# A threshold search on one NeuronCore: two bits a round on three engines, or one bit a round on ScalarE

## The chip, the cores and the metric

The kernel runs on one core of a Trainium2 chip. A core has TensorE (PE; its weight loads are listed as PEld), VectorE (DVE), ScalarE (ACT), GpSimd (POOL) and SyncE (SP), which issues most DMAs. Each engine takes its instructions in the order in which they were put at compile time, and waits at an instruction until what it needs is there. The metric is the device time of one execution in microseconds (us); the time before is the median of three.

## The reference, cut to what matters

One decoder layer for a prompt of 1024 tokens and 8 sample sequences of 4 new tokens. Each sample query picks 256 of its 8192 cached positions and 4 new ones by an indexer's score, and attends only to these:

```python
s = jnp.einsum('bqhd,bsd->bqhs', qi, ki) * (D_IDX ** -0.5)
score = jnp.einsum('bqh,bqhs->bqs', wi, jax.nn.relu(s))
score = jnp.where(valid, score, -jnp.inf)
top_val, top_idx = lax.top_k(score, topk)        # topk = 256
...
kg = flat_k[phys_row]; vg = flat_v[phys_row]     # gather the chosen keys and values
o = softmax(q @ kg + bias) @ vg
```

Beside this branch stand the prompt's own top-256 attention, a retention branch (eight heads, chunks of 128 tokens), the gates, the output projection, and a gated per-layer embedding. All of it is in fp32.

## The kernel before

The kernel is one stream of work in about five stages: norm and indexer projections; the remaining projections with the indexer scores of prompt and sample; the retention branch (a loop over four pairs of heads, `hp` 0 to 3, lines 1361 to 1418); the attention branch (a loop over eight query blocks `qb`, lines 1471 to 1531); and the output projections. The order on each engine is made at compile time: a scheduler goes through the program with estimated durations and gives an engine, when it comes free, the ready instruction of the highest priority. Work that is traced inside `tc.high_priority()` goes ahead of what is ready beside it. The order is fixed then; on the chip an engine waits if its next instruction is not ready.

The part that the change touches is `bisect_sample` (`bss`), which finds for each of the 32 sample queries the 256th largest score. The scores of a query lie on four partitions, 2080 columns each (tile `Xt`, `NX` = 2080). Their upper 16 bits are turned into unsigned keys (`su`, in the code `u16`), a first search finds the upper 16 bits of the threshold, the keys are then made from the lower 16 bits, and a second search finds these. A search of `before` goes through 8 rounds of two bits. In a round three thresholds are counted:

- two by ScalarE (`signs`, line 844): an ACTIVATE with `Sign` over all 2080 columns, its threshold as bias, and the sum of the signs into a column of `sgn`;
- the middle one by VectorE (line 883), in three pieces of 704, 688 and 688 columns, each followed by a small instruction (line 887) that carries the sum on;
- TensorE adds up the four partitions of a query with one small matmul of `groupr` and `sgn` (`totals`, line 849; the result is `stot`);
- ScalarE takes the signs of the three totals (line 893, with their sum in `up`) and makes the next two thresholds from `up` and two prepared values `pre` (line 865); GpSimd prepares those (line 870), and VectorE updates the middle one (line 894).

So a round is a chain ACT and DVE, PE, ACT, and the next round cannot start before it. Between the searches stands one more count with one pass (line 907). After the searches come two counts on VectorE (lines 836 and 928), each with a total on TensorE.

What follows on the threshold is `sample_select` (`ss`): it compares all scores with it, ranks them by scans, and in eleven steps of three queries (lines 1179 to 1199; tile `psl`) makes the row numbers `idx` of the chosen keys from step functions `oh`. The gathers (line 1086) fetch those rows, and `sample_attn` (`sa`) attends to them, interleaved with the prompt's attention by `more`, which sets its pace. All of `bss` and `ss` is traced with high priority, from `steps`, which stands after each projection block of the retention loop:

```python
with tc.high_priority():
    step(bss if hp == 0 else ss)
if hp == 0:
    step(bp, 2)
```

A generator's `yield` ends a step. `bss` yields after every round; what is left of it at `hp` 1 is traced at once. `bp` is the prompt's own threshold search, whose last part (scans and masks of the six query blocks, lines 698 to 712) runs on VectorE while the sample search starts. The small results `stot` share one PSUM bank that is kept over the retention and the attention stage (`kept`, tags `t` and `s`).

Of the kernel before, what the change touches and what calls it, by code (L numbers as in the profile page):

```python
# [10 lines left out]
F32 = mybir.dt.float32  # L11
F32R = mybir.dt.float32r
BF16 = mybir.dt.bfloat16
I32 = mybir.dt.int32
U16 = mybir.dt.uint16
AF = mybir.ActivationFunctionType
ALU = mybir.AluOpType
# [5 lines left out]
NS = 32  # L23
# [93 lines left out]
CW = _CW["onehot"][0]  # L117
# [3 lines left out]
def tile_step(ctx: ExitStack, tc: tile.TileContext, I, O):  # L121
    nc = tc.nc
# [21 lines left out]
    def bank(name, tag="b"):  # L144
        if tag in kept.get("tags", ()):
            return kept["pool"].tile([128, 512], F32, tag="s", bufs=1, name=name)
        return psum["pool"].tile([128, 512], F32, tag=tag, bufs=psum["bufs"][tag], name=name)
# [568 lines left out]
    def step(gen, n=1):  # L716
        for _ in range(n):
            next(gen, None)
# [49 lines left out]
    for b in range(8):  # L768
        rls = []
        for a in range(2):  # L770
# [4 lines left out]
            for up in range(2):  # L775
# [9 lines left out]
                for u2 in range(2):  # L785
                    nc.tensor.matmul(po[u2 * 64:u2 * 64 + 64, :], qbd[:, b, :], kT[:, u2 * 512:u2 * 512 + 512],  # L786
                                     start=True, stop=True)
# [16 lines left out]
    NX = 2048 + NS  # L804
    stk = ExitStack()

    def bisect_sample():


        V = nc.vector  # L810
        ss_ = stk.enter_context(pool("sst", side="right"))
        Xt = ss_.tile([128, NX], F32, name="Xt")
        u16 = ss_.tile([128, NX], U16, name="su16")
        jk = ss_.tile([128, NX], BF16, name="sjk")
# [5 lines left out]
        nc.gpsimd.memset(Xt[:, 2048:], LOW)  # L820
        V.tensor_copy(Xt[:NS, 2048:], newsc)
        bits = ss_.tile([128, 2], I32, name="sbits")
        nc.sync.dma_start(jk.bitcast(F32)[:, :128], I["const"][:, CW + 384:CW + 512])
        groupr = ss_.tile([128, 128], F32R, name="groupr")
        nc.gpsimd.tensor_copy(groupr, jk.bitcast(F32)[:, :128])
        group = groupr.bitcast(F32)
        cand, gb = (bits[:, i:i + 1] for i in range(2))
        sm = ss_.tile([128, 11], F32, name="ssm")
        cnt, sg, ng, c65, tu, v, need, te, k1, k2, bias = (sm[:, i:i + 1] for i in range(11))
        sgn = ss_.tile([128, 4], F32R, name="sgn")  # L830
        ct = cand.bitcast(F32)
        q1 = slice(0, NS)

        def count(thr, op):

            V.tensor_scalar(jk, Xt, thr, None, op0=op, op1=ALU.add, accum_out=cnt)
            t = bank("stot", "t")[:, 0:1]
            nc.tensor.matmul(t, group, cnt, start=True, stop=True)
            return t

        def signs(src, bias, j):

            with nc.allow_low_precision(reason="whole numbers up to NX"):
                nc.scalar.activation(jk, src, AF.Sign, bias=bias, accum_out=sgn[:, j:j + 1])  # L844

        def totals():

            t = bank("stot", "t")[:, 0:4]
            nc.tensor.matmul(t, groupr, sgn, start=True, stop=True)
            return t  # L850

        def search(src, k, mid):


            s = float(1 << 14)
            b = None
            V.memset(mid, 2 * s - 0.5)
            pre = ss_.tile([128, 4], F32, tag="pre", bufs=2, name="pre")
            for j in range(2):
                nc.gpsimd.memset(pre[:, j:j + 1], 0.5 - (3 - 2 * j) * s)  # L860
            for r in range(8):
                if r:
                    b = pre[:, 2:4]
                    for j in range(2):
                        nc.scalar.activation(b[:, j:j + 1], up, AF.Identity, bias=pre[:, j:j + 1], scale=-2.0 * s)
                        signs(src, b[:, j:j + 1], j)
                    if r < 7:
                        pre = ss_.tile([128, 4], F32, tag="pre", bufs=2, name="pre")
                        for j in range(2):
                            nc.gpsimd.tensor_scalar(pre[:, j:j + 1], b[:, j:j + 1], 0.75 * s * (1 - 2 * j), None,  # L870
                                                    op0=ALU.add)
                else:
                    for j in range(2):
                        signs(src, pre[:, j:j + 1], j)
                    p0, pre = pre, ss_.tile([128, 4], F32, tag="pre", bufs=2, name="pre")
                    for j in range(2):
                        nc.gpsimd.tensor_scalar(pre[:, j:j + 1], p0[:, j:j + 1], 0.75 * s * (1 - 2 * j), None,
                                                op0=ALU.add)
                c2 = ss_.tile([128, 5], F32, tag="c2", bufs=2, name="c2")
                part = -float(NX)  # L880
                for j, c, w in ((0, 0, 704), (1, 704, 688), (2, 1392, 688)):
                    jv = ss_.tile([128, 704], BF16, tag="jv", bufs=1, name="jv")
                    V.tensor_scalar(jv[:, :w], src[:, c:c + w], mid, None, op0=ALU.is_ge, op1=ALU.add,
                                    accum_out=c2[:, j:j + 1])
                    to = c2[:, 3 + j:4 + j] if j < 2 else sgn[:, 2:3]
                    with nc.allow_low_precision(reason="whole numbers up to NX"):
                        V.tensor_scalar(to, c2[:, j:j + 1], 2.0, part, op0=ALU.mult, op1=ALU.add)
                    part = to
                t = totals()

                st = ss_.tile([128, 4], F32, tag="st4", bufs=2, name="st4")
                up = st[:, 3:4]
                nc.scalar.activation(st[:, 0:3], t[:, 0:3], AF.Sign, bias=k, accum_out=up)
                V.scalar_tensor_tensor(mid, up, s / 2, mid, op0=ALU.mult, op1=ALU.add)
                s /= 4
                yield

        hi16 = Xt.bitcast(U16).rearrange("p (n two) -> p n two", two=2)
# [3 lines left out]
        V.tensor_scalar(lw, hi16[:, :, 1], float(1 << 15), float((1 << 15) - 1), op0=ALU.is_ge, op1=ALU.mult)  # L902
        V.scalar_tensor_tensor(u16, lw, 1 << 15, hi16[:, :, 1], op0=ALU.bitwise_xor, op1=ALU.bitwise_xor)  # L903
        yield
        yield from search(u16, k1, tu)
        V.tensor_scalar(bias, tu, -1.0, -0.5, op0=ALU.mult, op1=ALU.add)
        signs(u16, bias, 0)
        t = totals()[:, 0:1]
        V.tensor_scalar(k2, t, float(8 * NX - 2 * TOPK + 1), None, op0=ALU.add)
        V.tensor_scalar(ng, tu, float(1 << 15), None, op0=ALU.is_lt)  # L910
        V.tensor_scalar(c65, ng, 65535.0, None, op0=ALU.mult)
# [4 lines left out]
        V.tensor_scalar(ng, ng, 98303.0, -32768.0, op0=ALU.mult, op1=ALU.add)  # L916
        V.scalar_tensor_tensor(tu, tu, sg, ng, op0=ALU.mult, op1=ALU.add)
        yield
        yield from search(u16, k2, v)
        V.scalar_tensor_tensor(v, v, sg, c65, op0=ALU.mult, op1=ALU.add)  # L920
        V.tensor_copy(cand, tu)
        V.tensor_copy(gb, v)
# [2 lines left out]
        tot = count(ct, ALU.is_gt)  # L925
# [1 line left out]

        V.tensor_scalar(jk[:, :2048], Xt[:, :2048], ct, None, op0=ALU.is_equal, op1=ALU.add, accum_out=cnt)
        tot = bank("stot", "t")[:, 0:1]
        nc.tensor.matmul(tot, group, cnt, start=True, stop=True)  # L930
        V.tensor_copy(te, tot)
        tf = ct[q1]
        need, te = need[q1], te[q1]
        for src, dst in ((tf, tq), (need, nq)):
            t = bank("tbc", "t")
            nc.tensor.transpose(t[:, :NS], src.to_broadcast([NS, 128]), ident[:NS, :NS])
            V.tensor_copy(dst, t[:, :NS])
        xn = Xt[:NS, 2048:]
        sel, eq, rk = (jk.bitcast(F32)[:NS, i * NS:i * NS + NS] for i in range(3))
        V.tensor_scalar(sel, xn, tf, None, op0=ALU.is_gt)  # L940
        V.tensor_scalar(eq, xn, tf, None, op0=ALU.is_equal)
        V.tensor_tensor_scan(rk, eq, eq, te, op0=ALU.add, op1=ALU.bypass)
# [6 lines left out]
    bss = bisect_sample()  # L949
# [390 lines left out]
    ss = sample_select()  # L1340
# [13 lines left out]
    def steps(hp):  # L1354

        with tc.high_priority():
            step(bss if hp == 0 else ss)
        if hp == 0:
            step(bp, 2)

    for hp in range(4):
# [24 lines left out]
        for tb in range(8):  # L1386
# [3 lines left out]
            vv, sg = take_vg(pt, 128, tb, hp, f"{hp}_{tb}")  # L1390
            sgs.append(sg)
            qk = qks[tb]
            r, qkT, sm = chunk_mm(qk, vv, tb, 128, tri, hp)
# [77 lines left out]
    for qb in range(8):  # L1471
# [4 lines left out]
        w = min(n, 256)  # L1476
# [266 lines left out]
```

## Time and profile before

| | |
|---|---|
| time, median of 3 runs | 1080.19 us (1079.3 to 1080.88) |
| profiled execution, its own time | 1084.95 us |
| its span in the profile | 1083.1 us |
| TensorE busy, matmuls | 1005.3 us, 93% |
| VectorE, ScalarE, GpSimd busy | 765.1, 572.4, 292.4 us |
| mean granted TensorE clock | 0.964 of full speed |

All rows come from the one profiled execution; its time is 4.76 us above the median of the runs. An engine's busy share over the span is a mean over stages: the windows below show stretches of the span by themselves. Idle time matters where the engine that sets the end is the idle one.

### The profile page before, as it was taken

What the parts mean: (1) busy time and instruction counts of PE and PEld (TensorE: products, weight loads), DVE (VectorE), ACT (ScalarE), POOL (GpSimd) and SP (SyncE); (2) the same over time, 40 slices, a digit from 0 to 9 for tenths busy, and PEclk for the clock granted to TensorE, in tenths of its full rate; (3) what the DMA queues carried; (4) which work ended last, traced back from release to release, by engine and by line L of the source; (5) the groups of instructions that cost most, each with busy time, mean ns of one, the idle gap of its engine ahead of it and who ended that gap; (6) DMA issues with size and microseconds to landing.
All of it is one profiled execution on the core that took longest, in us unless ns stands there. A gap on an engine that the chain in (4) does not pass through costs nothing.

```text
span 1083.1 us, 20067 instructions
## 1 busy us (share of the span) xinstructions
PE 1005.3 (93%) x7377; PEld 845.4 (78%) x7377; DVE 765.1 (71%) x2262; ACT 572.4 (53%) x1216; POOL 292.4 (27%) x301
## 2 busy tenths in 40 slices
PE   3899997988998889999999986899999799999998
PEld 2899997766776788888888954566665799999998
DVE  6847778989889998968769879677663622683332
ACT  5545564976798356877832335555554432442210
POOL 3102223111201532424425215544331421122110
PEclk9999999989999999999999975899999899999999
DMA  8211235536343311300321544434211511332211
GB/s 285 65 59 50 78 107 176 180 116 203 125 161 103 74 40 40 80 18 26 79 81 25 141 119 110 133 87 115 58 50 61 144 60 40 115 125 81 84 41 41
DMA packets 98308, 102.24 MB, mean 94 GB/s; under 512 B 21346, under 2 KB 88386, under 8 KB 95906
## 3 DMA queue, kind: packets, MB, share of 16 engines
q1 hardware_dynamic: 92450, 74.74, 23.2%
q0 software_dynamic: 5760, 26.22, 7.8%
q8 instruction: 58, 0.95, 0.4%
q14 instruction: 40, 0.33, 0.1%
HBM read 79.25 MB, written 21.68 MB: 93 GB/s over the span
## 4 chain that ended last, share of the span: by engine, by line
PE 67%; DVE 14%; issue 6%; ACT 6%; DMA 4%; POOL 2%; SPq 0%; POOLq 0%; DVEq 0%; ACTq 0%
PE pb L252 4%; PE pb L253 4%; PE pb L254 4%; PE pg L262 3%; PE pg L264 3%; PE pg L263 3%; PE ob L1519 3%; PE ptp L1511 2%; PE pvg L262 2%; PE po L262 2%; PE po L263 2%; PE pvg L264 2%; PE po L264 2%; PE pox L786 2%; PE pvg L263 2%
## 5 line engine op out<-in xcount | busy, mean ns | idle before, releaser
L1086 POOL DMA_INDIRECT kvs<-in_cache_kv,idx x64 | 63.2, 987 | 87.1 <-ACT pT L1516 39.2
L262 PE MATMUL pqk<-whi_qkb,xh 128*128 128x256 f32 x256 | 74.3, 290 | 3.5 <-DVE rp L975 3.2
L262 PE MATMUL po<-whi_o,yTh 128*128 128x256 f32 x256 | 74.0, 290 | 3.9 <-DVE x L1606 3.4
L262 PE MATMUL pvg<-whi_vgb,xh 128*128 128x256 f32 x256 | 75.2, 294 | 1.1 <-ACT sg L988 1.1
L264 PE MATMUL pvg<-whi_vgb,xl 128*128 128x256 f32 x256 | 74.7, 292 | 0.0
L264 PE MATMUL pqk<-whi_qkb,xl 128*128 128x256 f32 x256 | 73.9, 289 | 0.0
L263 PE MATMUL pvg<-wlo_vgb,xh 128*128 128x256 f32 x256 | 73.7, 288 | 0.0
L264 PE MATMUL po<-whi_o,yTl 128*128 128x256 f32 x256 | 73.7, 289 | 0.0
L263 PE MATMUL pqk<-wlo_qkb,xh 128*128 128x256 f32 x256 | 73.5, 287 | 0.0
L263 PE MATMUL po<-wlo_o,yTh 128*128 128x256 f32 x256 | 73.3, 287 | 0.0
L262 PE MATMUL pg<-whi_g,yTh 128*128 128x256 f32 x256 | 72.7, 284 | 0.0
L264 PE MATMUL pg<-whi_g,yTl 128*128 128x256 f32 x256 | 72.3, 282 | 0.0
L263 PE MATMUL pg<-wlo_g,yTh 128*128 128x256 f32 x256 | 72.2, 282 | 0.0
L844 ACT ACTIVATE sjk<-su,pre 128x2080 bf16<-128x2080 uint16 x32 | 64.8, 2025 | 5.0 <-DVE su L903 4.7
L1504 ACT ACTIVATE L<-L,mn 128x128 f32<-128x128 f32 (+7 forms) x64 | 49.5, 775 | 20.9 <-DVE mn L1501 17.7
L1700 DVE TENSOR_TENSOR sgm<-pu,sgm 128x256 f32<-128x256 f32 x32 | 13.6, 424 | 64.5 <-PE pu L264 55.3
L497 DVE SCALAR_TENSOR_TENSOR score<-r,wi,score 128x384 f32<-128x384 f32 (+5 forms) x42 | 44.2, 1052 | 20.7 <-ACT r L493 19.6
L262 PEld LDWEIGHTS pqk<-whi_qkb,xh 128*128 128x128 f32 x256 | 49.0, 191 | 7.4 <-issue 4.9
L262 PEld LDWEIGHTS po<-whi_o,yTh 128*128 128x128 f32 x256 | 49.9, 195 | 5.6 <-DVE x L1606 3.6
L1516 ACT COPY pT<-ptp 128x512 f32<-128x512 f32 x54 | 31.3, 581 | 41.9 <-PE ptp L1511 33.4
L648 DVE TENSOR_SCALAR_CACHE_REDUCE jk<-mask,cf 128x768 bf16<-128x768 uint16 (+1 forms) x64 | 51.9, 812 | 2.0
L1699 ACT ACTIVATE sgm<-pg 128x256 f32<-128x256 f32 x32 | 12.3, 383 | 75.9 <-PE pg L264 67.8
(525 smaller groups left out, 3471.3 us busy)
## 6 DMA issues: line engine op xcount, KB each, us to landing
wraw_qkb<-in_w_in SPq DMA_DIRECT2D x16, 256.0 KB
wraw_vgb<-in_w_in SPq DMA_DIRECT2D x16, 256.0 KB
wraw_o<-in_w_out SPq DMA_DIRECT2D x8, 512.0 KB
qas<-qas_d SPq DMA_DIRECT2D x8, 512.0 KB
xr<-in_x_prompt SPq DMA_DIRECT2D x8, 512.0 KB
wraw_g<-in_w_ple_gate SPq DMA_DIRECT2D x8, 512.0 KB
out_y_prompt<-sgm SPq DMA_DIRECT2D x32, 128.0 KB
qas_d<-qst SPq DMA_DIRECT2D x8, 384.0 KB
```

The costliest lines, as they stand in the source:

```text
L252: nc.tensor.matmul(pt[:m, :n], wh, xh[:, k, ts], start=(k == 0), stop=False)
L253: nc.tensor.matmul(pt[:m, :n], wh, xl[:, k, ts], start=False, stop=False)
L254: nc.tensor.matmul(pt[:m, :n], wl, xh[:, k, ts], start=False, stop=(k == KC - 1))
L262: nc.tensor.matmul(pt[:, :n], ah, hi[:, k, :n], start=(k == 0), stop=False)
L263: nc.tensor.matmul(pt[:, :n], ah, lo[:, k, :n], start=False, stop=False)
L264: nc.tensor.matmul(pt[:, :n], al, hi[:, k, :n], start=False, stop=(k == kc - 1))
L497: nc.vector.scalar_tensor_tensor(sc, r[:, :n], wi[:, qb, h:h + 1], sc, op0=ALU.mult, op1=ALU.add)
L648: V.tensor_scalar(jk[:, :n], src[:, o:o + n], t, None, op0=op, op1=ALU.add, accum_out=cnt[:, j:j + 1])
L844: nc.scalar.activation(jk, src, AF.Sign, bias=bias, accum_out=sgn[:, j:j + 1])
L1086: return nc.gpsimd.indirect_dma_start(out=dst, out_offset=None, in_=kvflat, in_offset=bass.IndirectOffsetOnAxis(ap=idx, axis=0))
L1504: behind[0] = nc.scalar.activation(L[:, :n], L[:, :n], AF.Exp, bias=least, scale=-1.0, accum_out=sm[:, i4:i4 + 1])
L1519: nc.tensor.matmul(ob[64 * o:64 * o + 64, :256], vtok[:, kb, kv * 64:kv * 64 + 64], pT[:, o * 256:o * 256 + 256], start=(kb == 0), stop=(k ...
```

## The change

The search goes through 16 rounds of one bit. A round counts one threshold with one ScalarE pass; TensorE makes the total; ScalarE takes its sign (`st`) and moves the threshold (`bias`) by it. VectorE and GpSimd have no part in a round any more. `bss` now yields twice as often, and `steps` takes two of its steps at `hp` 0 instead of one. The constant `group` gets a tile of its own instead of borrowing the count's output tile (it is loaded with its neighbour, 256 columns instead of 128), and so do the three small tiles at the end (`sel`, `eq`, `rk`). The kept PSUM bank, the step functions of `ss` and the pace of the gathers stay as they are.

```diff
-        nc.sync.dma_start(jk.bitcast(F32)[:, :128], I["const"][:, CW + 384:CW + 512])
+        group = ss_.tile([128, 2, 128], F32, name="group")
+        nc.sync.dma_start(group, I["const"][:, CW + 384:CW + 640])
...
-        sgn = ss_.tile([128, 4], F32R, name="sgn")
+        sgn = ss_.tile([128, 2], F32R, name="sgn")
...
-        def search(src, k, mid):
-            s = float(1 << 14)
-            V.memset(mid, 2 * s - 0.5)
-            ...
-            for r in range(8):
-                if r:
-                    b = pre[:, 2:4]
-                    for j in range(2):
-                        nc.scalar.activation(b[:, j:j + 1], up, AF.Identity, bias=pre[:, j:j + 1], scale=-2.0 * s)
-                        signs(src, b[:, j:j + 1], j)
-                    if r < 7:
-                        pre = ss_.tile([128, 4], F32, tag="pre", bufs=2, name="pre")
-                        for j in range(2):
-                            nc.gpsimd.tensor_scalar(pre[:, j:j + 1], b[:, j:j + 1], 0.75 * s * (1 - 2 * j), None, op0=ALU.add)
-                ...
-                for j, c, w in ((0, 0, 704), (1, 704, 688), (2, 1392, 688)):
-                    V.tensor_scalar(jv[:, :w], src[:, c:c + w], mid, None, op0=ALU.is_ge, op1=ALU.add, accum_out=c2[:, j:j + 1])
-                    ...
-                        V.tensor_scalar(to, c2[:, j:j + 1], 2.0, part, op0=ALU.mult, op1=ALU.add)
-                t = totals()
-                nc.scalar.activation(st[:, 0:3], t[:, 0:3], AF.Sign, bias=k, accum_out=up)
-                V.scalar_tensor_tensor(mid, up, s / 2, mid, op0=ALU.mult, op1=ALU.add)
-                s /= 4
-                yield
+        def signs(src):
+            nc.scalar.activation(jk, src, AF.Sign, bias=bias, accum_out=sgn[:, 0:1])
+            t = bank("stot", "t")[:, 0:2]
+            nc.tensor.matmul(t, groupr, sgn, start=True, stop=True)
+            return t[:, 0:1]
+
+        def search(src, k):
+            V.memset(bias, 0.5 - (1 << 15))
+            for bit in range(15, -1, -1):
+                t = signs(src)
+                nc.scalar.activation(st, t, AF.Sign, bias=k)
+                if bit:
+                    nc.scalar.activation(bias, st, AF.Identity, bias=bias, scale=-float(1 << bit) / 2)
                 yield
...
-            step(bss if hp == 0 else ss)
+            step(bss if hp == 0 else ss, 2 if hp == 0 else 1)
```

## Rows read from the trace of the kernel before

**Rows 1.** The page's part 1: busy us, share of the span, instructions by engine

```profile
PE 1005.3 (93%) x7377; PEld 845.4 (78%) x7377; DVE 765.1 (71%) x2262; ACT 572.4 (53%) x1216; POOL 292.4 (27%) x301
```

**Rows 2.** Windows: stretch, its us, busy us of each engine (instructions), granted clock, DMA

```profile
core 0: us, PE busy (x) PEld busy (x) DVE busy (x) ACT busy (x) POOL busy (x), PEclk, DMA share, GB/s
354.00:420.00 66.00, 57.83 (x442) 52.66 (x441) 65.25 (x159) 30.39 (x66) 24.71 (x29) 0.95 0.18 43
420.00:547.00 127.00, 125.51 (x1048) 113.36 (x1048) 101.15 (x382) 101.89 (x227) 48.23 (x84) 1.00 0.20 52
633.00:668.00 35.00, 21.50 (x141) 13.90 (x138) 34.34 (x160) 12.46 (x32) 8.51 (x9) 0.56 0.38 107
668.00:700.00 32.00, 28.20 (x172) 19.23 (x172) 21.71 (x87) 18.73 (x56) 19.68 (x18) 0.79 0.51 143
```

**Rows 3.** VectorE between 370 and 547 us, grouped by line: busy, mean ns

```profile
L883 DVE TENSOR_SCALAR_CACHE_REDUCE jv<-su,ssm 128x688 bf16<-128x688 uint16 (+1 forms) x48 | 44.3, 923 | 0.1
L883 DVE DVE_READ_ACCUMULATOR jv<-su,ssm 128x1 f32 x48 | 3.9, 81 | 0.0
L887 DVE TENSOR_SCALAR c<-c 128x1 f32<-128x1 f32 x32 | 5.6, 175 | 0.3
L887 DVE TENSOR_SCALAR sgn<-c 128x1 fp32r<-128x1 f32 x16 | 3.3, 204 | 0.2
L894 DVE SCALAR_TENSOR_TENSOR ssm<-st,ssm 128x1 f32<-128x1 f32 x16 | 4.5, 279 | 4.0 <-ACT st L893 3.7
```

**Rows 4.** What TensorE waited for between 354 and 420 us, us in total

```profile
PE stot L849 <- DVE sgn L887: 3.2, 1, 3.2
```

**Rows 5.** ScalarE in order of time: start, us, line, operation

```profile
481.76 2.06 ACT L844 ACTIVATE sjk<-su,pre 128x2080 bf16<-128x2080 uint16 x1
483.69 0.21 ACT L844 ACTIVATION_READ_ACCUMULATOR sjk<-su,pre 128x1 fp32r x1
486.59 0.26 ACT L893 ACTIVATE st<-stot,ssm 128x3 f32<-128x3 f32 x1
487.04 0.48 ACT L865 ACTIVATE pre<-st,pre 128x1 f32<-128x1 f32 x2
```

**Rows 6.** The totals on TensorE, in order of time

```profile
393.59 0.27 PE L849 MATMUL stot<-sgn,groupr 128*128 128x4 f32 x1 [3.20 <-DVE sgn L887]
...
459.33 0.25 PE L849 MATMUL stot<-sgn,groupr 128*128 128x4 f32 x1
...
468.86 0.25 PE L849 MATMUL stot<-sgn,groupr 128*128 128x4 f32 x1
...
477.83 0.25 PE L849 MATMUL stot<-sgn,groupr 128*128 128x4 f32 x1
...
486.28 0.27 PE L849 MATMUL stot<-sgn,groupr 128*128 128x4 f32 x1
```

**Rows 7.** Lines on the tile of keys: count, ns, first and last start

```profile
L844 ACT ACTIVATE sjk<-su,pre x32: 2012/2028/2057, 368.6 to 541.5; 128x2080 bf16<-128x2080 uint16 x32
L844 ACT ACTIVATE sjk<-su,ssm x1: 2030/2030/2030, 464.2 to 464.2; 128x2080 bf16<-128x2080 uint16 x1
```

**Rows 8.** Lines on the tile of totals: count, ns, first and last start

```profile
L849 PE MATMUL stot<-sgn,groupr x17: 165/251/272, 377.1 to 546.2; 128*128 128x4 f32 x17
```

**Rows 9.** GpSimd and VectorE at the search's start, in order of time

```profile
360.95 0.31 POOL L825 CAST groupr<-sjk 128x128 fp32r<-128x128 f32 x1 [3.49 <-DMA sjk<-in_const]
361.29 1.49 DVE L902 TENSOR_SCALAR sjk<-Xt 128x2080 uint16<-128x2080 uint16 x1 [0.18 <-POOL groupr L825]
```

**Rows 10.** VectorE between 633 and 668 us, grouped by line

```profile
L1185 DVE TENSOR_SCALAR oh<-slot,sm 128x256 bf16<-128x256 bf16 x29 | 7.0, 284 | 0.1
L1191 DVE TENSOR_TENSOR le<-psl,cst 128x384 bf16<-128x384 f32 (+1 forms) x11 | 5.9, 533 | 0.0
L1196 DVE TENSOR_REDUCE row<-le 128x6 f32<-128x384 bf16 (+1 forms) x11 | 5.8, 523 | 0.0
```

**Rows 11.** What ScalarE waited for between 370 and 547 us

```profile
ACT st L893 <- PE stot L849: 17.3, 10, 4.0
```

More of the change, by code (lines that the diff above doesn't have):

```diff
@@ L822, in bisect_sample @@
         bits = ss_.tile([128, 2], I32, name="sbits")
-        nc.sync.dma_start(jk.bitcast(F32)[:, :128], I["const"][:, CW + 384:CW + 512])
+        group = ss_.tile([128, 2, 128], F32, name="group")
+        nc.sync.dma_start(group, I["const"][:, CW + 384:CW + 640])
         groupr = ss_.tile([128, 128], F32R, name="groupr")
-        nc.gpsimd.tensor_copy(groupr, jk.bitcast(F32)[:, :128])
-        group = groupr.bitcast(F32)
+        nc.gpsimd.tensor_copy(groupr, group[:, 0])
         cand, gb = (bits[:, i:i + 1] for i in range(2))
-        sm = ss_.tile([128, 11], F32, name="ssm")
-        cnt, sg, ng, c65, tu, v, need, te, k1, k2, bias = (sm[:, i:i + 1] for i in range(11))
-        sgn = ss_.tile([128, 4], F32R, name="sgn")
+        sm = ss_.tile([128, 12], F32, name="ssm")
+        cnt, sg, ng, c65, tu, v, need, te, k1, k2, st, bias = (sm[:, i:i + 1] for i in range(12))
+        sgn = ss_.tile([128, 2], F32R, name="sgn")
         ct = cand.bitcast(F32)
@@ L837, in count @@
             t = bank("stot", "t")[:, 0:1]
-            nc.tensor.matmul(t, group, cnt, start=True, stop=True)
+            nc.tensor.matmul(t, group[:, 0], cnt, start=True, stop=True)
             return t
-        def signs(src, bias, j):
+        def signs(src):
             with nc.allow_low_precision(reason="whole numbers up to NX"):
-                nc.scalar.activation(jk, src, AF.Sign, bias=bias, accum_out=sgn[:, j:j + 1])
-        def totals():
-            t = bank("stot", "t")[:, 0:4]
+                nc.scalar.activation(jk, src, AF.Sign, bias=bias, accum_out=sgn[:, 0:1])
+            t = bank("stot", "t")[:, 0:2]
@@ L849, in totals @@
             nc.tensor.matmul(t, groupr, sgn, start=True, stop=True)
-            return t
-        def search(src, k, mid):
-            s = float(1 << 14)
-            b = None
-            V.memset(mid, 2 * s - 0.5)
-            pre = ss_.tile([128, 4], F32, tag="pre", bufs=2, name="pre")
-            for j in range(2):
-                nc.gpsimd.memset(pre[:, j:j + 1], 0.5 - (3 - 2 * j) * s)
-            for r in range(8):
-                if r:
-                    b = pre[:, 2:4]
-                    for j in range(2):
-                        nc.scalar.activation(b[:, j:j + 1], up, AF.Identity, bias=pre[:, j:j + 1], scale=-2.0 * s)
-                        signs(src, b[:, j:j + 1], j)
-                    if r < 7:
[L868 to L880, printed above, removed]
-                for j, c, w in ((0, 0, 704), (1, 704, 688), (2, 1392, 688)):
[L882 to L886, printed above, removed]
-                        V.tensor_scalar(to, c2[:, j:j + 1], 2.0, part, op0=ALU.mult, op1=ALU.add)
-                    part = to
-                t = totals()
-                st = ss_.tile([128, 4], F32, tag="st4", bufs=2, name="st4")
-                up = st[:, 3:4]
-                nc.scalar.activation(st[:, 0:3], t[:, 0:3], AF.Sign, bias=k, accum_out=up)
-                V.scalar_tensor_tensor(mid, up, s / 2, mid, op0=ALU.mult, op1=ALU.add)
-                s /= 4
@@ L904, in bisect_sample @@
         yield
-        yield from search(u16, k1, tu)
+        yield from search(u16, k1)
+        V.scalar_tensor_tensor(tu, st, 0.5, bias, op0=ALU.mult, op1=ALU.subtract)
         V.tensor_scalar(bias, tu, -1.0, -0.5, op0=ALU.mult, op1=ALU.add)
-        signs(u16, bias, 0)
-        t = totals()[:, 0:1]
+        t = signs(u16)
         V.tensor_scalar(k2, t, float(8 * NX - 2 * TOPK + 1), None, op0=ALU.add)
@@ L918, in bisect_sample @@
         yield
-        yield from search(u16, k2, v)
+        yield from search(u16, k2)
+        V.scalar_tensor_tensor(v, st, 0.5, bias, op0=ALU.mult, op1=ALU.subtract)
         V.scalar_tensor_tensor(v, v, sg, c65, op0=ALU.mult, op1=ALU.add)
@@ L929, in bisect_sample @@
         tot = bank("stot", "t")[:, 0:1]
-        nc.tensor.matmul(tot, group, cnt, start=True, stop=True)
+        nc.tensor.matmul(tot, group[:, 0], cnt, start=True, stop=True)
         V.tensor_copy(te, tot)
@@ L938, in bisect_sample @@
         xn = Xt[:NS, 2048:]
-        sel, eq, rk = (jk.bitcast(F32)[:NS, i * NS:i * NS + NS] for i in range(3))
+        sel = ss_.tile([NS, NS], F32, name="nsel")
+        eq = ss_.tile([NS, NS], F32, name="neq")
+        rk = ss_.tile([NS, NS], F32, name="nrk")
         V.tensor_scalar(sel, xn, tf, None, op0=ALU.is_gt)
```

## Prediction

> **What bounds the kernel now.** I read the page's shares first, then the windows, then the waits in those stretches that are not full, and last the search's own lines in order of time. The reader is to see that TensorE sets the end nearly everywhere: 1005.3 us busy of a span of 1083.1 [rows 1]. What the change can win or lose lies where TensorE is not full. The windows [rows 2] show two such places around the search. Between 354 and 420 us TensorE is busy for 57.83 of 66 us while VectorE is busy for 65.25: VectorE sets the pace there. Between 420 and 547 us TensorE is full (125.51 of 127). Between 633 and 668 us VectorE is full (34.34 of 35), and TensorE has 21.50 us of work, at a mean granted clock of 0.56, so mostly at the lower of its two levels, 1.2 GHz. What fills VectorE there is the end of the sample branch's selection: the three kinds of line of its eleven steps take 7.0 + 5.9 + 5.8 = 18.7 us [rows 10]. The selection starts on the threshold, so its place in time hangs on when the search ends. The search's totals on TensorE run from 377.1 to 546.2 us [rows 8], on passes that start at 368.6 [rows 7].
>
> The question is thus whether 32 one-bit rounds end earlier or later than 16 two-bit rounds, and what that and the freed VectorE are worth.
>
> **Passes and VectorE work.** The ScalarE passes are 33 before (32 and the single one) [rows 7] and 33 after (16 + 16 and the single one): ScalarE counts as long as before. VectorE loses 44.3 + 5.6 + 3.3 + 4.5 = 57.7 us in 16 rounds [rows 3], 3.6 us a round. From 354 to 420 about four rounds lie (the first two totals are 16.5 us apart [rows 6, 8]), so 14.4 us of VectorE work leave a stretch in which TensorE idles for 66 - 57.83 = 8.2 us. The gain there is 0 to 8.2 us; of the waits that name their cause the search's own is 3.2 us [rows 4]. I take 4. It does not reach the end whole: TensorE gets to 633 us sooner, but there it waits for VectorE's selection, which hangs on the search. I carry half: **-2 us**. From 420 to 547 us the freed VectorE time is worth nothing, since TensorE is full and hides it; it would be worth up to 127 - 125.5 = 1.5 us.
>
> By the Trainium skill ("ScalarE: Activation LUTs", Rules for kernel authors), simple elementwise work belongs on VectorE, which it calls up to about three times faster per element in 16-bit types. That speaks against this move, but the trace doesn't bear it out for this count: 923 ns for some 690 columns is 1.34 ns a column on VectorE [rows 3], 2028 ns for 2080 is 0.98 on ScalarE [rows 7]. By the page 2080 columns on VectorE would be an estimated 0.7 us, by the row they are 2.8.
>
> **The start.** The key tile's first instruction writes over the borrowed tile and so waited for GpSimd's copy, which had waited 3.49 us for the constant; VectorE itself idled for only 0.18 [rows 9], since other work stood ahead. With a tile of its own the chain starts 0 to 3.5 us earlier. I take 2: first pass at 366.5. The load is one DMA as before, of twice the bytes. It stands at the same place in SP's queue, and only the first total needs it.
>
> **One round.** From a pass's start to the end of its sum's read: 483.69 + 0.21 - 481.76 = 2.14 us [rows 5]. From the total's start to the sign's: 486.59 - 486.28 = 0.31 [rows 5, 6]. From the sign to the threshold update 0.45 (now with a read of a sum that falls away), and one update of the two that take 0.48 together, about 0.3 [rows 5]. A round's own chain is 3.2 us. To it comes TensorE: the total stands at a fixed place in a full queue, so it starts when TensorE has done what stands ahead. Call this wait w. At 393.59 it is nothing (TensorE stood and waited for VectorE). At 486.28 it is 486.28 - 483.90 = 2.4. After the one count that already is a single pass (464.2 + 2.14 = 466.3) the total starts at 468.86, 2.5 us later [rows 5 to 7]. So a one-bit round T lies between 3.2 us (w = 0) and 5.7 (w = 2.5), or 6.0 with another 0.3 of ScalarE's other work between. For w I take the row that is nearest, the single pass: **T = 5.7 us**.
>
> **The whole chain.** Between the last total of the first search and the first of the second lie 477.83 - 459.33 = 18.5 us [rows 6]; one pass less makes 16.5. The last total then starts at 366.5 + 2.14 + w + 16.5 + 30 T = 385.1 + w + 30 T. With T = 5.7 and w = 2.5 that is 558.6 us, 12 later than 546.2. With T = 3.2 and w = 0 and the earliest start (365.1) it is 480, 66 earlier. With T = 6.0 and no gain at the start it is 570, 24 later. The break-even is T = 5.3.
>
> **What 12 us later cost.** Of the 18.7 us of selection in the 35 us from 633 to 668, 12/35, some 6.4, move behind 668. VectorE idles for 32 - 21.71 = 10.3 us between 668 and 700 [rows 2], so at best they are hidden, and the cost is nothing; at worst, all 6.4 stand ahead of the attention blocks' own VectorE work, and TensorE waits for them. TensorE has work for 28.2 of those 32 us, so there is little slack to hide in. I take **+4 us**.
>
> **The added totals.** 33 instead of 17 on TensorE, in a stretch where it is full: 16 more at up to 0.25 us each [rows 8] is 4 us; next to other matmuls they overlap, and half is what I take: **+2 us**. GpSimd's prepared values go and cost nothing either way: GpSimd is busy for 48.2 of 127 us there [rows 2]. The three small tiles at the end and the second step per block in `steps` move no instruction's data; the chain is behind the order of the program anyway (its last total lies far behind the eight blocks that trace it), and I put them at nothing.
>
> **Sum.** -2 + 2 + 4 = +4 us on the profiled execution's 1084.95, so 1089; the median of the runs is 4.76 us lower, so **1084 us**. Its own range is 1077 to 1094. A measurement of this kernel can tell about 0.2%, 2.2 us, from no change.
>
> **Rival 1, the other side: w shrinks with the round.** TensorE's wait may not be a fixed price. The order is made from estimated times; if a shorter round puts fewer matmuls between two totals, w shrinks too. For it: in the two-bit rounds VectorE's third of the count may have been what pushed the total back in that order. Against it: the single pass shows 2.5 us, and it is one pass long. It decides below T = 5.3. At T = 4.2 (w = 1) the last total starts at 512, 34 us earlier, and the whole selection leaves the stretch from 633 to 668. VectorE then has 34.3 - 18.7 = 15.6 us there and TensorE at most 21.5, so 13.5 to 19.4 us go; I take 15. With the relief of 5 now carried whole and 2 for the totals: -18, so **1062 us**.
>
> **Rival 2: T between 4.8 and 5.5.** The search ends within some 15 us ahead or 6 behind where it did, and the relief of VectorE remains: 3 us less, **1077 us**.
>
> **Rival 3: ScalarE's waits reach TensorE.** ScalarE waited for a total in 10 of 16 rounds, 17.3 us, 1.7 each [rows 11]; behind such a wait stand its copies of TensorE's results, which later matmuls need. With twice as many round trips that is 17 us more of a standing ScalarE. For it: ScalarE is busy for 101.9 of 127 us between 420 and 547 [rows 2], so little slack is left to catch up. Against it: TensorE is full in that stretch, so these waits did not reach it. If half of the 17 did, 8 us come on top of the +4: **1092 us**. The Trainium skill ("TensorE: Matmul & The Clock Gate", the table at its head) calls ScalarE's queue strictly first in, first out, as this needs. The trace agrees that instructions start in one order there; what it cost in the changed kernel no row here shows.
>
> **Chances.** The forecast (T from 5.5 to 6) 0.45; rival 1 0.25; rival 2 0.20; rival 3 0.10. Below 1064 lies about half of rival 1, above 1094 a part of rival 3 and of the forecast's own tail; what remains, 1064 to 1094, holds 8 in 10. Faster by over 0.2%: nearly all of rival 1, two thirds of rival 2, a tenth of the forecast, 0.42. Slower: seven tenths of the forecast and rival 3, 0.45. Within 0.2%: 0.13.
>
> **What would show each step right or wrong.** The totals' starts: 33 of them, the second 5.7 us behind the first if w is fixed, 4 if it shrinks, and the last near 559. The windows: from 354 to 420 VectorE no longer full and TensorE above 58; the stretch around 633 to 668 with VectorE full and a clock near 0.56 some 12 us later (forecast), or gone (rival 1). ScalarE's wait for totals near 35 us, and waits of TensorE for ScalarE's copies if rival 3 holds. The forecast is wrong if the last total lies before 540, or if the selection's shift costs nothing because the attention blocks have room for it.

## The result, and the profile after

The changed kernel takes 1085.08 us (median of 5 runs, 1084.23 to 1089.61) against 1080.19 for the kernel before, 4.9 us more, where the prediction had 3.8 (1084.0). The ratio over all runs is 1.0055 with a 95% interval of 1.0032 to 1.0079, so it is slower, by about half a per cent. The profiled execution took 1084.45 us of its own, 0.6 below its median; that of the kernel before was 4.8 above its median. The two spans, 1082.6 and 1083.1, can therefore not be set against each other as they are; experiment e1 shows where most of the difference came from.

The page, part 1, after (answers to [rows 1]; VectorE gave up 41.8 us, where the prediction took off 57.7):

```profile
PE 1002.9 (93%) x7393; PEld 849.1 (78%) x7393; DVE 723.3 (67%) x2104; ACT 577.3 (53%) x1216; POOL 273.6 (25%) x269
```

The windows after (answer to [rows 2], with the same columns):

```profile
354.00:420.00 66.00, 55.36 (x413) 51.71 (x413) 53.67 (x115) 33.76 (x70) 20.50 (x20) 0.87 0.14 30
420.00:547.00 127.00, 127.00 (x1058) 113.86 (x1051) 63.27 (x264) 95.11 (x212) 43.21 (x62) 1.00 0.20 52
633.00:668.00 35.00, 25.11 (x144) 16.53 (x144) 31.94 (x148) 16.13 (x46) 3.46 (x4) 0.50 0.29 72
668.00:700.00 32.00, 29.36 (x212) 20.44 (x210) 31.10 (x133) 20.29 (x57) 14.72 (x14) 0.93 0.41 117
```

VectorE is no longer full from 354 to 420 us (53.67 of 66), and yet TensorE did less there than before, 55.36 against 57.83, at a lower granted clock. From 668 to 700 VectorE is now full: the selection reaches into it.

What TensorE waited for between 354 and 420 us (answers to [rows 4]), and behind it VectorE and TensorE in order of time at the search's start (answers to [rows 9]):

```profile
PE pqk L262 <- DVE rp L940: 6.7, 1, 6.7
PE ret L1360 <- DVE sm L970: 3.3, 1, 3.3
```

```profile
354.41 0.42 DVE L707 TENSOR_SCALAR eq<-score,tbits 128x384 bf16<-128x384 f32 x1
357.55 1.25 DVE L864 TENSOR_SCALAR sjk<-Xt 128x2080 uint16<-128x2080 uint16 x1 [2.73 <-DMA Xt<-xt_d]
...
359.68 0.39 DVE L938 TENSOR_TENSOR rp<-pqk,cst 128x256 f32<-128x256 f32 x1
360.00 0.27 DVE L939 TENSOR_TENSOR rp<-pqk,cst 128x128 f32<-128x128 f32 x1
360.19 2.31 DVE L865 SCALAR_TENSOR_TENSOR su<-sjk,Xt 128x2080 uint16<-128x2080 uint16 x1
362.42 0.28 DVE L940 TENSOR_TENSOR rp<-pqk,cst 128x128 f32<-128x128 f32 x1
```

```profile
355.45 0.28 PE L262 MATMUL pqk<-whi_qkb,xh 128*128 128x256 f32 x1
355.57 0.28 PE L263 MATMUL pqk<-wlo_qkb,xh 128*128 128x256 f32 x1
...
355.91 0.27 PE L960 MATMUL ret<-cst,qk 128*128 128x128 f32 x1
362.85 0.55 PE L262 MATMUL pqk<-whi_qkb,xh 128*128 128x256 f32 x1 [6.67 <-DVE rp L940]
363.20 0.41 PE L263 MATMUL pqk<-wlo_qkb,xh 128*128 128x256 f32 x1
363.41 0.41 PE L264 MATMUL pqk<-whi_qkb,xl 128*128 128x256 f32 x1
```

The key tile's two long instructions (L864, L865) now stand ahead of the rotary products `rp`, which read the projection's PSUM bank and so set it free for TensorE's next projection. L864 waits 2.73 us for its keys, L865 takes 2.31 us between the second and the third product of one `rp`, and TensorE stands for 6.67 us. The row of 3.3 us is a later wait for VectorE, inside the retention products.

The stretch ahead of the change differs in length between the two profiles, so the keys are timed from the first retention projection: here that projection and the second key instruction of before, then the projection after.

```profile
346.83 1.07 PE L271 MATMUL pqk<-wraw_qkb,xs 128*32 128x256 f32 x16
364.26 4.28 DVE L903 SCALAR_TENSOR_TENSOR su<-sjk,Xt 128x2080 uint16<-128x2080 uint16 x1
```

```profile
343.13 1.07 PE L271 MATMUL pqk<-wraw_qkb,xs 128*32 128x256 f32 x16
```

The first key instruction starts 14.5 us behind the projection before (at 361.29 [rows 9]) and 14.4 after. The tile of its own brought it forward by next to nothing: the wait for the constant was gone, but the keys came only then. (Over all the kernels below it is 13.7 to 14.4 us with a tile of its own, 14.3 to 15.2 with the borrowed one.) The first pass does start 2.4 us sooner (19.4 us behind the projection against 21.8), mostly because the second key instruction took 2.31 us instead of 4.28. That doesn't need the tile: in e5 and e10 below, with the borrowed tile, it took 2.31 us too.

The passes, the totals, ScalarE's wait for them between 362 and 572 us (answer to [rows 7, 8, 11]) and one round (answers to [rows 5]):

```profile
L844 ACT ACTIVATE sjk<-su,ssm x33: 2022/2031/2039, 362.5 to 564.9; 128x2080 bf16<-128x2080 uint16 x33
```

```profile
L846 PE MATMUL stot<-sgn,groupr x33: 164/165/271, 369.1 to 569.2; 128*128 128x2 f32 x33
```

```profile
ACT ssm L855 <- PE stot L846: 27.8, 20, 3.0
```

```profile
480.54 0.26 ACT L855 ACTIVATE ssm<-stot,ssm 128x1 f32<-128x1 f32 x1 [0.41 <-PE stot L846]
480.84 0.29 ACT L857 ACTIVATE ssm<-ssm 128x1 f32<-128x1 f32 x1
481.17 2.03 ACT L844 ACTIVATE sjk<-su,ssm 128x2080 bf16<-128x2080 uint16 x1
483.10 0.19 ACT L844 ACTIVATION_READ_ACCUMULATOR sjk<-su,ssm 128x1 fp32r x1
...
485.88 0.26 ACT L855 ACTIVATE ssm<-stot,ssm 128x1 f32<-128x1 f32 x1 [1.11 <-PE stot L846]
```

Here the sum is read by 483.29 and the total starts at 485.65: a wait of 2.4 us on TensorE in a round of 5.3. The last total starts at 569.2, 23 us later than before, or 27 counted from the first retention projection.

### The profile page after: what moved, and what is told of

Read it like the earlier page. It is cut to its first block, busy times and chain, and to the rows that moved or that the text cites. A ratio compares the mean times of both kernels' runs of the same rounds, so it can differ in the third digit from the quotient of the medians.

```text
span 1082.6 us, 19902 instructions
## 1 busy us (share of the span) xinstructions
PE 1002.9 (93%) x7393; PEld 849.1 (78%) x7393; DVE 723.3 (67%) x2104; ACT 577.3 (53%) x1216; POOL 273.6 (25%) x269
## 4 chain that ended last, share of the span: by engine, by line
PE 72%; DVE 14%; ACT 6%; DMA 4%; issue 2%; POOL 1%; SPq 0%; ACTq 0%; DVEq 0%; POOLq 0%
PE pb L252 4%; PE pb L253 4%; PE pb L254 4%; PE ob L1484 3%; PE ptp L1476 3%; PE pg L262 3%; PE pg L264 3%; PE pg L263 3%; PE pvg L263 3%; PE pvg L262 2%; PE pvg L264 2%; PE po L262 2%; PE po L264 2%; PE po L263 2%; PE pqk L263 2%
## 5 line engine op out<-in xcount | busy, mean ns | idle before, releaser
L844 ACT ACTIVATE sjk<-su,ssm 128x2080 bf16<-128x2080 uint16 x33 | 67.0, 2031 | 3.2 <-DVE su L865 1.8
L1469 ACT ACTIVATE L<-L,mn 128x128 f32<-128x128 f32 (+7 forms) x64 | 49.6, 777 | 21.8 <-DVE mn L1466 21.5
L493 ACT ACTIVATE r<-si 128x384 f32<-128x384 f32 (+5 forms) x48 | 36.3, 759 | 29.9 <-PE si L351 28.7
```

The source lines that it names most:

```text
L493: nc.scalar.activation(r[:, :n], s[:, :n], AF.Relu)
L1469: behind[0] = nc.scalar.activation(L[:, :n], L[:, :n], AF.Exp, bias=least, scale=-1.0, accum_out=sm[:, i4:i4 + 1])
```

## The experiments

Times differ by chip and hour (the kernel before had medians of 1080 to 1085 us beside these runs), so each run is given as its ratio to the kernel before on the same chip. Since every edit makes the planner write the whole order anew, I also read from each trace where TensorE lost its time. The measure: for every matmul the distance to the next one's start, less what a matmul of its form takes at its quickest (the lower fifth of the distances of that form over all fourteen traces), summed from the first retention projection and read when TensorE has done 100, 180 and 210 us of such work (at some 483, 586 and 625 us of the span). What runs ahead of 346 us, where nothing was changed, is left out of it. The work itself differs by 0.6 us at most, and by 0.4 between before and changed. Each row of lost time is one profiled execution. The last 1800 matmuls, whose order (by output and shape) is the same in all fourteen, took 210.6 to 216.0 us, so differences of 1 or 2 us can be the execution's own.

```
                              slots   TensorE's lost us at work of     ratio to before
                              ready     100    180    210     end      (95% interval)
before                        667.5    34.1   58.8   67.8   210.7
e1  before again              666.3    34.1   60.5   69.4   209.9   0.9985 (0.9960, 1.0010)
changed                       685.7    39.7   60.3   67.0   213.4   1.0055 (1.0032, 1.0079)
e2  changed, borrowed tile    706.3    37.3   58.4   68.8   273.0   1.0549 (1.0512, 1.0586)
e3  before, own tile          676.3    40.7   71.0   79.4   224.2   1.0097 (1.0059, 1.0135)
e4  changed, 12 rounds        668.9    40.4   62.3   69.2   213.4   1.0046 (1.0021, 1.0071)
e5  e2 with 12 rounds         671.5    36.5   59.4   68.8   215.9   1.0042 (1.0008, 1.0076)
e6  changed, 18 rounds        710.9    38.6   59.5   65.8   280.1   1.0615 (1.0564, 1.0665)
e7  changed, VectorE work     717.7    43.2   72.1   81.2   289.4   1.0642 (1.0589, 1.0696)
e8  first search one-bit      671.7    36.2   58.4   73.8   225.0   1.0071 (1.0040, 1.0102)
e9  before, 10 rounds         684.5    34.5   57.7   63.9   227.3   1.0165 (1.0120, 1.0209)
e10 before, 4 rounds          633.6    34.0   63.7   69.6   201.3   0.9887 (0.9845, 0.9929)
e11 changed, 8 rounds         664.7    39.4   67.5   74.7   215.0   1.0033 (1.0012, 1.0054)
e12 e7 with 10 rounds         679.7    42.4   74.0   82.2   221.4   1.0152 (1.0106, 1.0197)
```

"Slots ready" is the last matmul of the selection (`pcf`), in us of the span; the first retention projection starts between 342 and 350 us, and the slots shift with it. The rounds are those of the second search.

**e1, the kernel before again**, without an edit.

> The kernel before, unchanged, to see which part of its profiled 1084.95 us belongs to the program. Between 199 and 290 us the changed kernel's profile runs 3 us ahead on the same instructions in the same order, so I expect a span near 1078 to 1080 with those 3 us gone from there, and the stretch from 346 us on as in the first profile. Rival: the span is again near 1083 and the two profiles of before agree; then the 3 us are the program's.

The span is 1079.6, and its first retention projection starts at 344.0 instead of 346.8: of the 3.5 us between the two profiles, 2.8 were lost ahead of the change, by the execution and not by the program. From there on the two profiles of before agree within 0.8 us (210.7 and 209.9 lost). Against their mean the changed kernel loses 3.1 us.

**e2, the constant in the borrowed tile again.**

```diff
-        group = ss_.tile([128, 2, 128], F32, name="group")
-        nc.sync.dma_start(group, I["const"][:, CW + 384:CW + 640])
+        nc.sync.dma_start(jk.bitcast(F32)[:, :128], I["const"][:, CW + 384:CW + 512])
-        nc.gpsimd.tensor_copy(groupr, group[:, 0])
+        nc.gpsimd.tensor_copy(groupr, jk.bitcast(F32)[:, :128])
...
```

> The changed kernel with the constant loaded into the borrowed tile again, as before the change, so that the key tile's first instruction stands behind GpSimd's copy. Theory A (the start): with a tile of its own that instruction is put ahead on VectorE and waits there for its keys, TensorE stands 6.7 us behind it and then runs 5 us at half its clock; expects that wait gone and 1079 to 1082 us, 3 to 5 less than the changed kernel's 1085. Theory B (the late selection): the cost comes from the last total standing 23 us later; expects 1085 to 1088, since the search now starts later still.

Neither theory had 1143 us. The start is as theory A says: the long wait is gone, and 2.4 us less are lost at a work of 100. But the slots are ready 20 us later than in the changed kernel, at 706, and behind a work of 210 some 58 us more are lost. Of the 20 us the search makes only 4 (its last total starts at 573.1); the rest lies in the selection, whose order was written anew. How late slots cost time, e9 shows.

**e3, the kernel before with the tile of its own** (e2's diff the other way round).

> The kernel before with only the tile of its own for the constant. Theory A expects VectorE to wait some 2.7 us for the keys and TensorE 5 to 7 us near 356 to 363, and 1083 to 1085 us, 3 to 5 more than before's 1080. Theory B expects 1078 to 1080, since the search starts some 4 us earlier and nothing else changes.

Slower by 0.97%, more than theory A's 3 to 5 us. The wait near 356 is there (5.4 us for `rp`, and 4.5 for `sbd` behind it); 6.6 us more than before are lost by a work of 100 and, unlike in the changed kernel, 11 by 180: VectorE, which keeps its third of the counts here, doesn't catch up.

**e4, the changed kernel with 12 of 16 rounds in its second search**; the last total stands at 548.

```diff
-        def search(src, k):
+        def search(src, k, last=-1):
-            for bit in range(15, -1, -1):
+            for bit in range(15, last, -1):
-        yield from search(u16, k2)
+        yield from search(u16, k2, 3)
```

> The changed kernel with the last four of the sixteen rounds of the second search left out (the low four bits of the threshold are not searched, so its output isn't the reference's), which brings the last total some 23 us forward, to about 546 us, where it stood before. The start is untouched. Theory B expects 1078 to 1081 us, since the selection is back in its old place. Theory A expects 1084 to 1086: only four small totals and 8 us of ScalarE leave a stretch in which TensorE is full.

1.0046 against 1.0055, and the same 213.4 us lost: with the selection back in its old place nothing is won that can be told. Theory B, that the lateness makes the loss, falls: e4's whole interval lies above the 1078 to 1081 us it asked for. By the profiles some 2 us of it may be left (e4 loses 144.2 us behind a work of 210, the changed kernel 146.4); the intervals of the two ratios, taken together, leave room for up to 5.

**e5, both edits, the borrowed tile and 12 rounds.**

> The changed kernel with both edits of the runs before: the constant in the borrowed tile, and the last four rounds of the second search left out (the low four bits of the threshold are not searched, so its output isn't the reference's). Its VectorE should start the key tile where the kernel before does, and the last total should stand near 550 us, 23 us ahead of where it stood with the borrowed tile alone. Theory A (the start costs the changed kernel its 4 us, and the 57 us of the borrowed tile alone came from a selection too late for the gathers): 1076 to 1082 us, below the changed kernel with 12 rounds by 4 to 8, and no long waits of TensorE behind 700 us. Rival (the borrowed tile makes a bad order by itself): still 20 us or more above before.

The 57 us (273.0 lost against 215.9) are gone, so they came with the late slots, not from the tile by itself. But the ratio is 1.0042: theory A's 4 to 8 us below e4 are not seen either, though the two intervals together would let 4 pass. At a work of 100 e5 has lost 3.9 us less than e4, at 210 only 0.4 less.

**e6, two idle rounds more**: `[16] * 2` ahead of the bits, with a step of zero.

> The changed kernel with two rounds more in the second search that change nothing (their step is zero), so the last total stands some 11 to 12 us later, near 581, and all else is as in the changed kernel. If the lateness has a cliff (the changed kernel's slots were 18 us later than before's and cost nothing, those of the borrowed tile 35 us later and cost 57): 1100 to 1145 us. If lateness costs what I put on it in the prediction, a third of a us for each: 1088 to 1090. If it costs nothing and the 57 us came from elsewhere: 1085 to 1087.

A cliff: slots at 711 us, 1.0615. The last total stands 10 us later than in the changed kernel (579.6), the slots 25: here too the selection itself came out longer. A price for each us of lateness, as the prediction had it, is the wrong form.

**e7, VectorE's work put back** into all 33 rounds, for nobody.

```diff
...
+            V.tensor_scalar(jv, src[:, :1040], 4.0, None, op0=ALU.is_ge, op1=ALU.add, accum_out=jc[:, 0:1])
             t = bank("stot", "t")[:, 0:2]
```

> The changed kernel with a count over 1040 columns by VectorE in each of the 33 rounds, whose result nothing uses: 33 times some 1.4 us, 47 us, about what the change had taken from VectorE. The rounds themselves don't wait for it. If the relief of VectorE is worth what I carried: 2 to 5 us more than the changed kernel, 1087 to 1090. If it is worth nothing, since TensorE is full where it lies: 1084 to 1087. If it is worth far more than I thought: 1092 and above.

Far into the third case, since it too went over the cliff (last total at 585, slots at 718). What it says of the relief stands ahead of that: 72.1 us lost at a work of 180 against 60.3.

**e8, one bit a round in the first search alone**, borrowed tile.

> The kernel before (borrowed tile) with one bit a round in the first search alone and two bits a round in the second. VectorE is relieved in the stretch from 354 to 420 us, where it was full, and the search should end some 8 us later than in the kernel before (about 555), less than in the changed kernel. If the relief there is worth something and the start is what cost: 1075 to 1080 us, below before. If the relief is worth nothing: 1079 to 1083. Above 1085 if the order of the rest comes out worse for a reason that I don't have.

1.0071, the third case, the one without a reason. VectorE is relieved and the start is good (36.2 and 58.4 lost, no better than before), but 6 us more are lost between 180 and 210 and 9 more behind it. Why this order comes out worse I have not found.

**e9 and e10, the kernel before with two idle two-bit rounds more, and with four of eight**: the loop over `r` made longer (steps of zero) or shorter.

> The kernel before with two two-bit rounds more in the second search that change nothing (their steps are zero), so the last total stands some 17 us later, near 563, where the changed kernel's stands, with the start and VectorE's work a round as before. My prediction's price, a third of a us for each us of lateness: 1085 to 1087 us, 5 to 6 more than before's. If lateness of this size costs nothing, as the changed kernel's 12 rounds against 16 say: 1080 to 1082. If the cliff is met from 28 us on: 1080 to 1087 too; above 1100 only if it lies nearer.

> The kernel before with the last four of the eight two-bit rounds of the second search left out (the low eight bits of the threshold are not searched, so its output isn't the reference's): the last total some 35 us earlier, near 511. This is the place that my rival 1 lived on: if the selection leaves the stretch from 633 to 668 us, in which TensorE has half its work, 1062 to 1070 us, 10 to 18 less than before. If the order is made anew so that the selection lies as badly elsewhere: 1076 to 1081.

e9 lost 17 us for a last total 17 us later (563.8), three times the prediction's price, with slots ready at the same time as in the changed kernel (684.5 and 685.7), to which that cost next to nothing. Windows of e9, and of the changed kernel, from 700 to 720 us:

```profile
700.00:720.00 20.00, 3.53 (x13) 2.06 (x14) 3.70 (x17) 3.54 (x8) 12.30 (x13) 0.53 0.35 102
```

```profile
700.00:720.00 20.00, 17.81 (x124) 11.01 (x125) 13.53 (x53) 10.49 (x25) 15.13 (x17) 0.91 0.50 145
```

What TensorE waited for in e9 between 690 and 730 us, the two rows of VectorE and ScalarE ahead of the first wait's end, and GpSimd in order of time:

```profile
PE ob L1519 <- ACT pT L1516: 9.4, 1, 9.4
PE pkg L1263 <- issue: 8.5, 1, 8.5
```

```profile
716.88 0.42 DVE L1501 CUSTOM_DVE_ANT_0 L<-sa,mask 128x256 f32<-128x256 f32 x1 [10.80 <-remote]
717.59 0.59 ACT L1516 COPY pT<-ptp 128x512 f32<-128x512 f32 x1 [9.90 <-remote]
```

```profile
700.25 0.94 POOL L1086 DMA_INDIRECT kvs<-in_cache_kv,idx  x1 [0.30 <-issue]
701.50 0.95 POOL L1086 DMA_INDIRECT kvs<-in_cache_kv,idx  x1 [0.30 <-issue]
702.75 0.95 POOL L1086 DMA_INDIRECT kvs<-in_cache_kv,idx  x1 [0.30 <-DMA kvs<-in_cache_kv,idx]
```

The reader is to see all engines idle but GpSimd, which issues one gather every 1.25 us: what paced the gathers has long passed, so they go as fast as they can, and the transposes of gathered rows (`pkg`) stand in TensorE's fixed order where the planner thought the rows would be. TensorE stands there for 16.5 of 20 us, at a mean granted clock of 0.53. In the changed kernel the gathers run as late and as close, but other attention work stands there. So the cliff looks to be not a time but a place in the order. That it is the gathers that TensorE waits for is read from the order and from GpSimd's row, since the wait's own row says only "issue". The other wait, 9.4 us for ScalarE's copy `pT`, points the same way: VectorE and ScalarE had stood for some 10 us themselves, for a signal whose sender the rows don't name; in the trace's semaphore events it is TensorE's, at 716.86, and the gather issued at 714.01 had landed at 716.43. No run here moved the gathers alone. In e2 all engines but GpSimd idle in the same way from 710 to 750 us (TensorE busy for 12.4 of 40), though its wait rows name other lines.

e10 gained 1.13%, 12 us: an earlier selection is worth something here, though the four rounds left out also take VectorE's counts with them. The stretch that rival 1 was about is less short of work for TensorE:

```profile
633.00:668.00 35.00, 25.32 (x147) 17.61 (x146) 27.49 (x115) 23.21 (x65) 11.07 (x9) 0.66 0.55 155
```

TensorE is busy for 25.3 us there instead of 21.5 [rows 2], at 0.66 instead of 0.56.

**e11, the changed kernel with 8 rounds**, last total at 526.

> The changed kernel with eight of the sixteen rounds of the second search (the low eight bits of the threshold are not searched, so its output isn't the reference's): the last total some 46 us earlier, near 523. With rival 1's price, 13 to 19 us for a selection out of the stretch from 633 to 668: 1066 to 1072 us. If lateness up to the cliff costs nothing and earliness earns nothing, as 12 rounds against 16 say: 1083 to 1086, with TensorE's wait of 5 to 7 us near 356 to 363 still there.

1.0033: the earlier selection earns the changed kernel next to nothing, because its beginning now falls into the stretch where TensorE was full (67.5 lost at 180 instead of 60.3; from 570 to 600 us TensorE is busy for 25.0 us, in the changed kernel for 30.0) and the start's loss stays (39.4 at 100).

**e12, e7 with 10 rounds**, so that no gather is late (last total at 548.0).

> The changed kernel with the unused VectorE counts again (1040 columns in each round), and the second search cut to 10 rounds (the low six bits of the threshold are not searched, so its output isn't the reference's) so that the last total stands near 550 us and the gathers are not late. To be set against the changed kernel with 12 rounds (1.0046 of before), whose last total stands at 548. If the relief of VectorE is worth what TensorE's lost time says, some 5 us between 480 and 585 us: 1.008 to 1.012 of before, 1090 to 1094 us. If it is worth nothing and the 70 us of the same work in 16 rounds came from the lateness alone: 1.003 to 1.006, 1084 to 1088.

1.0152 against e4's 1.0046: the relief of VectorE is worth 11 us in the changed kernel (from the two intervals 6 to 17), not 5. Its slots are 11 us later than e4's, but the difference stands ahead of them: 74.0 us are lost at a work of 180 against 62.3.

## Why the sum was right and its terms were not

**The round: right at its median, too short in sum.** The wait w of a total was to stay at 2.5 us: its median over 33 totals is 2.5. T was to be 5.7: the median of the 30 rounds is 5.7. Rival 1's mechanism, that w shrinks, is out. Rival 2, a T of 4.8 to 5.5, is out with it. But the mean round is 6.2, above the 6.0 that the prediction had as the most, because seven took over 7 us (in one TensorE itself stood for VectorE, in four ScalarE was at other work when the total came, in two w was 4). The 30 rounds took 187.2 us instead of 171. The stretch between the two searches took 12.9 instead of 16.5 and the first total came 2 us sooner than added up, so the last one stands at 569.2, not 558.6.

**The start: the step that failed.** It was costed on the search's chain alone, as 2 us gained by a wait for the constant that falls away: "VectorE itself idled for only 0.18 [rows 9], since other work stood ahead". The constant was not the only thing that came late: with it out of the way, the key instruction still started 14.4 us behind the first projection, against 14.5. That the first pass was 2.4 us sooner all the same is luck, since it came from a shorter instruction. And the other work was the cover. With a tile of its own, the planner puts the key instruction ahead of that work; the wait for its keys, hidden until then, and two long instructions now stand ahead of `rp`, and TensorE waits. All seven kernels with the tile of their own have lost 38.6 to 43.2 us at a work of 100, those with the borrowed tile 34.0 to 37.3. The changed kernel loses 5.6 us here, but the tile makes only a part of it: 2.4 (against e2) to 3.9 (e4 against e5). With the borrowed tile and a one-bit first search (e2, e5, e8) 36.2 to 37.3 are lost, with two bits 34.0 to 34.5, so 2 to 3 us come with the one-bit search. In those three TensorE waits 1.9 to 3.0 us for VectorE's sum `sh_vg` between 380 and 400 us, a wait that the kernel before doesn't have; whether that is all of it is not shown.

**VectorE's relief: right in sign, too small, and in another place.** I took 4 us from 354 to 420, carried 2, and gave the rest nothing. Up to a work of 100 there is no relief to be seen. Between 100 and 210 the changed kernel wins back 7.2 us (27.3 lost against 34.5, the mean of the two profiles of before). And it is no term by itself. At a work of 180 the borrowed tile has 57.7 to 60.5 us lost with VectorE's counts (before, e1, e9) and 58.4 to 59.4 without (e2, e5): worth nothing. The tile of its own has 71.0 to 74.0 with such counts (e3, e7, e12) and 59.5 to 62.3 without (changed, e4, e6): worth 12. (e10 and e11 are left out, since their selection already falls ahead of that mark.) The change's one part makes a backlog on VectorE, and its other part frees the time to clear it.

**The totals: too dear.** 16 more cost TensorE 0.4 us of work by the measure above, not 2: the row's 0.25 us each is a length that overlaps.

**The lateness: right in size, wrong in form.** Behind a work of 210 the changed kernel loses 4.7 us more than before (146.4 against 141.7), where the prediction put 4. About 1 us of this lies in the last 1800 matmuls, whose order did not change. But the whole lateness cost some 2 of it by e4, 17 us cost e9 17, and e2, e6 and e7 fall over the cliff. The third of a us that I paid for each us is no property of the kernel.

So +3.1 us of lost time are +5.6 at the start, -7.2 up to 620 us, +4.7 behind it; by the prediction, up to 633 nothing in sum and +4 behind. That the first two nearly cancel was not foreseen, and the lateness came out at its price although the search ended 27 us later and not 12: the sum is right by luck. (The medians differ by 4.9 us, 1.8 more than the profiles' lost time; the changed kernel's own runs spread over 5.4.) **Rival 3** is out: ScalarE waited 27.8 us for totals (some 35 expected), and between 420 and 633 us TensorE waited for ScalarE in no row. **Rival 1's place** is real, but e10 earned 12 us where I priced 15 for the stretch and 18 in all.

What stays open: e5 has neither the start's wait nor the lateness, and is 1.0042. Which part of the change carries the last 4 us to the end is not settled: orders made anew differ by that much for reasons that these runs don't tell apart (e8). No run undoes the three small tiles at the end or the second step per block, which the prediction put at nothing; the changed kernel and all its variants have both. And no version here that keeps the reference's 32 bits beats the kernel before.

## What to carry to other kernels

A wait that costs nothing because other work stands ahead of it is a reason to ask what a planner will do once the wait's cause is gone: it may put the instruction ahead of that work, and then the next wait in line, here for the keys, stops whoever is queued behind it. A freed engine is worth what its backlog costs, so price it together with the edit that makes the backlog. And delay of a branch that feeds gathers had no price per us here: in some orders it cost next to nothing, and in others TensorE stood for tens of us.

## What the runs showed of the hardware

TensorE's 6.67 us without work began at 356 us; from 358 to 368 us its granted clock stood at the lower of its two levels, 1.2 GHz. The projections that came at 362.85 follow each other every 0.21 us, those ahead of the wait every 0.12, so a wait of 6.7 us costs more than its length. In e9 the clock was at that level for 20.5 us around 700 to 720.

The same instructions in the same order, ahead of 346 us, took 344.0 us in one profile of the kernel before and 346.8 in another, and its median moved from 1080 to 1085 us between chips and hours. Differences of a few us between two profiles say little until the stretch that no edit touched has been taken off.
